# Sample scores of four sequences in one run of four column tiles, and a rearranged start, in a hybrid decoder step

## The chip, the cores and the metric

The kernel runs on one core of a Trainium2 chip, in one launch. The metric is device time in microseconds of one execution; lower is better. The engines are named as in the profile: PE is TensorE (PEld its weight loads), DVE is VectorE, ACT is ScalarE, POOL is GpSimd, SP is SyncE, which only issues DMAs here.

## The reference, cut to what matters

One step of a two-layer decoder for a prompt of 512 tokens and for 8 sample sequences of 4 new tokens each, which have 512 cached positions in pages. D_MODEL is 2048. Layer A runs NSA attention (compressed, selected and window branches) and GLA side by side on one input projection; layer C is HGRN2. Everything is float32.

```python
def layer_a(x, norm_w, w_in, ..., past_kv, win_buf, gla_s0, q_start):
    h = rmsnorm(x, norm_w)
    q, kv, g_br, z_a, q_b, k_b, v_b, lr_b, z_b = split_cols(h @ w_in, A_SIZES)
    ...
    buf = jnp.concatenate([win_buf, new_win], axis=1)
    win_state = buf[:, buf.shape[1] - wb:]
    ...
    o_a = nsa_attend(q, gates, full, win_kv, ...) * jax.nn.silu(z_a)
    log_a = jax.nn.log_sigmoid((lr_b @ gla_w2 + gla_b)) / GLA_GATE_NORM
    ...
    y = x + jnp.concatenate([o_a, o_b], axis=-1) @ w_out
    return y, new_rows, win_state, s_b
```

In `nsa_attend`, for the sample sequences, the selected branch takes all 512 cached positions of the pages (16 blocks of 64) and the window branch the 512 positions of `cache_win`:

```python
        s = jnp.einsum('qgrd,qgnkd->qgrnk', qg, ks)... * scale
        p_s = masked_softmax(s, ...)
        o_s = jnp.einsum('qgrm,qgmd->qgrd', p_s, vs...)
        s = jnp.einsum('qgrd,kgd->qgrk', qg, wk[:, 0]) * scale
        p_w = masked_softmax(s, wmask...)
        o_w = jnp.einsum('qgrk,kgd->qgrd', p_w, wk[:, 1])
```

Besides the two outputs y, the step returns the new cache rows, the window state (for a sample sequence the last 508 rows of `cache_win` and 4 new ones) and the recurrent states.

## The kernel before, in words

**The stream of products.** Prompt and sample tokens stand side by side as 544 columns. `stream` (L296) walks over all weight blocks of the program in one fixed order: the input projection of layer A, its output projection, then the two of layer C. A block has 128 output columns (`gemm_block`, L355) and 16 tiles kt of 128 inputs. Each kt takes six products of 128x272: the weight's high part with the high part of x, with the low part of x, and the weight's low part with the high part of x, each for two halves of the tokens. So a block is 96 products, four pieces of 24. A raw weight tile (`wr`, 512 KB, two pieces) is loaded by a DMA of SP's queue; `split_to` (L314) turns it, some pieces ahead of PE, into `wh` (ACT) and `wl` (DVE). There are NRAW = 3 raw tiles, and a new load is issued as soon as one has been split. Blocks 0 and 1 are interleaved piece by piece; later blocks follow one by one.

**The planner.** All other work is written as Python generators that yield what they wait for. After each kt the stream calls `pump`, and the planner emits what is ready by its own clock. So the order of instructions on each engine is fixed when the program is built; on the chip an engine takes its instructions in that order. Tiles come from a heap of 55 (`self.g`) or from a second pool of 17 that is reopened by stage (`self.r`, `open_r`).

**The start.** `constants` (L409) has POOL build masks. `load_x` (L600) issues five DMAs for a column of 512 of x (four of 128 prompt rows, one of the 32 sample rows); `load0` and `load1` in `layer_a` put the four columns between the first four weight loads, and `small_loads` (L510) puts nine small loads on SP's queue behind the first of them: seven into the tile `cvr` of norm weights and biases, the page table, and `per`. `input_task` (L612) transposes the five tiles of a column on PE in groups (16 kt in all), copies them to `res`, splits them into `xh` and `xl`, and stores `res` to DRAM. The products of piece n of blocks 0 and 1 wait for the flag `xc{n}`, a whole column. `constants2` (L534) transposes `cvr` after the second column.

**Copies of the window cache.** `win_task` (L592) moves 508 rows of `cache_win` to the output for each of 8 sequences: eight DMAs of 1016 KB from DRAM to DRAM, on POOL's queue, the first after the last mask, the others as POOL's order comes to them.

**The first blocks of layer A.** Blocks 0 to 3 are columns of kv; the results of 0 and 1 are copied out and scaled by `rstd` later (`early`), the others wait for `rstd`. Block 4 holds the GLA gate columns; `gl_load` zeroes a raw tile on POOL and fills it with two DMAs of SP's queue, of 1024 runs of 64 and 96 bytes. Meanwhile the compression (`cmp_prep` L1143, `cmp_block` L1184) loads cache pages (`cache_tile` L1125, `pg`), transposes and multiplies them.

**Decode** (L1388) handles the 8 sample sequences in two groups of four, for selected pages (`pg`) and window (`pw`), so four rounds. `fetch` (L1402) keeps up to PAGES = 9 tiles of keys and values on their way. Each round transposes the keys of a sequence and head g to a tile `kct` (128x512) and calls `scores` (L1473): one float32 product with 32 weight columns, `qd`, in the column tile of sequence b % 4:

```python
                self.mm(S[rows, :], self.qd[:, g, b, :], t[:, :TP], start=(g == 0), stop=(g == 1),
                        tile_position=(0, 32 * (b % 4)))
```

PE executes a float32 call as two instructions. A call is emitted one step late (`pend`), between the transposes of the next pair. Softmax, transposes to `ptd` and value products (256 columns, the same four column tiles) follow. After the last round `orow` is transposed into `odec`, and q times z becomes the rows of sample tokens in the inputs of the output projection.

Of the kernel before, what the change touches and what calls it, by code (L numbers as in the profile page):

```python
# [94 lines left out]
class Kern:  # L95
# [200 lines left out]
    def stream(self, blocks, pieces):  # L296

        nc = self.nc
        raws = []
        for b, i, j in pieces:  # L300
            if (b, i) not in raws:
                raws.append((b, i))
        raw_t, hl = {}, {}
        state = {"raw": 0, "free": 0, "split": 0}

        def load():
            while state["raw"] < min(state["free"] + NRAW, len(raws)):
                b, i = raws[state["raw"]]
                t = self.wp.tile([P, 1024], F32, name=self.nm("wr"), tag="wr", bufs=NRAW)
                b.load(i, t)  # L310
                raw_t[(b, i)] = t
                state["raw"] += 1

        def split_to(n):  # L314
            while state["split"] < min(n, len(pieces)):
                b, i, j = pieces[state["split"]]
                w = b.width
                t = raw_t[(b, i)][:, j * w:(j + 1) * w]
                hi = self.wp.tile([P, 512], F32R, name=self.nm("wh"), tag="wh", bufs=4)
                lo = self.wp.tile([P, 512], F32R, name=self.nm("wl"), tag="wl", bufs=4)  # L320
                nc.scalar.copy(hi[:, :w], t)
                self.tt(lo[:, :w], t, hi[:, :w].bitcast(F32), ALU.subtract)
                hl[(b, i, j)] = (hi, lo)
                state["split"] += 1
                if j == 1:
                    del raw_t[(b, i)]
                    state["free"] += 1
                    load()

        load()  # L330
        self.until("xc0")
        late = None
        for n, (b, i, j) in enumerate(pieces):
            split_to(n + 3)
            if i == 0 and j == 0:
                self.until(*(b.needs or ()))
                if b.pre:
                    b.pre()
            if b.ps is None:
                b.ps = self.psum_tile("gm", [P, 2, 512], 2)  # L340
            hi, lo = hl.pop((b, i, j))
            b.products(i * 2 + j, hi, lo, b.ps)
            if late is not None:
                late.evac(late.ps)
                late = None
            if i == b.nraw - 1 and j == 1:
                if b.now:
                    b.evac(b.ps)
                else:
                    late = b  # L350
        if late is not None:
            late.evac(late.ps)
            self.pump()

    def gemm_block(self, w, cols, xhl, evac, order=None, needs=None, ahead=None):  # L355

        nc = self.nc
        order = order or list(range(KT))
        c0, M = cols

        def load(i, t):
            k0 = order[8 * i]
            src = w[k0 * P:(k0 + 8) * P, c0:c0 + M].rearrange("(k p) c -> p k c", p=P)
            nc.sync.dma_start(t[:, :8 * M].rearrange("p (k c) -> p k c", k=8), src)

        def products(n, hi, lo, ps):
            if ahead:
                ahead(n, order)
            for q in range(4):
                kt = order[4 * n + q]  # L370
                xh, xl = xhl(kt)
                wh, wl = hi[:, q * M:(q + 1) * M], lo[:, q * M:(q + 1) * M]
                first, lastk = (n == 0 and q == 0), (n == 3 and q == 3)
                for lw, rx, f, l in ((wh, xh, first, False), (wh, xl, False, False), (wl, xh, False, lastk)):
                    for h in range(2):
                        self.mm(ps[:M, h, :TH], lw, rx[:, h * TH:(h + 1) * TH], start=f, stop=l)
                self.pump()

        return Block(load, 2, 4 * M, products, evac, needs)
# [130 lines left out]
    def small_loads(self):  # L510

        nc, a = self.nc, self.a
        rows = self.g("cvr", [P, P])
        q = nc.sync
        q.dma_start(rows[0:16, :], a["c_norm"].rearrange("o (k p) -> (o k) p", p=P))
        q.dma_start(rows[16:32, :], a["final_norm"].rearrange("(k p) -> k p", p=P))
        q.dma_start(rows[32:64, :], a["c_lb_logits"].rearrange("o (k p) -> (o k) p", p=P))
# [10 lines left out]
    def constants1(self):  # L528

        ps = self.bank()  # L530
        self.tr(ps[:, :16], self.rows0, self.ident[:16, :16])
        self.nc.vector.tensor_copy(self.w_a, ps[:, :16])

    def constants2(self):  # L534

# [55 lines left out]

    def win_task(self):  # L592

        for b in range(NB):
            yield self.later(30000.0)
            self.nc.gpsimd.dma_start(self.o["win_sample"][0, b, 0:508].rearrange("t s h d -> t (s h d)"),
                                     self.a["cache_win"][0, b, 4:512].rearrange("t s h d -> t (s h d)"))


    def load_x(self, c):  # L600

        nc, a = self.nc, self.a
        for i in range(5):
            t = self.g("xt", [P, 512])
            s = slice(c * 512, (c + 1) * 512)
            if i < 4:
                nc.sync.dma_start(t, a["x_prompt"][0, i * P:(i + 1) * P, s])
            else:
                nc.sync.dma_start(t[:TS], a["x_sample"].rearrange("b t d -> (b t) d")[:, s])
            self.xt[(c, i)] = t  # L610

    def input_task(self):  # L612
# [14 lines left out]
        for c in range(4):  # L627
# [5 lines left out]
            for q in range(4):  # L633
# [11 lines left out]
                nc.vector.scalar_tensor_tensor(lo, res, w, hi.bitcast(F32), op0=ALU.mult, op1=ALU.subtract)  # L645
                self.xhl[kt] = (hi, lo)
                self.store(self.xres[kt], res)
            self.flags.add(f"xc{c}")
            yield
            if c:  # L650
# [737 lines left out]
    def decode(self):  # L1388
        nc, ident, a = self.nc, self.ident, self.a
        yield from self.wait("ratt", "gates", "kv10", "kv11", "kvc00", "kvc01", "kvc10", "kvc11")  # L1390
        yield from self.wait(*[f"pu{h}" for h in range(DECODE_AFTER + 1)])
        yield self.at(self.qd)
        self.odec = self.g("odec", [P, 256])
        orow = self.r("orow", [P, 2, P])
# [73 lines left out]
        for gr, kind in items:  # L1468
# [6 lines left out]
                self.mm(S[rows, :], self.qd[:, g, b, :], t[:, :TP], start=(g == 0), stop=(g == 1),  # L1475
                        tile_position=(0, 32 * (b % 4)))

            pend = None
            for b in bs:
                ts = [pages[(kind, 0, b, hf)] for hf in range(2)]  # L1480
                for g in range(2):
                    yield self.at(*ts, banks=1)
                    ps = self.bank()
                    for pg in range(4):
                        self.tr(ps[:, pg * P:(pg + 1) * P], ts[pg // 2][:, pg % 2, g * P:(g + 1) * P], ident)
                    if pend:
                        yield self.at(pend[2], ps)
                    else:
                        yield self.at(ps)
                    t = self.r("kct")  # L1490
                    self.cp(t[:, :TP], ps)
                    if pend:
                        scores(*pend)
                    pend = (b, g, t)
                for hf in range(2):
                    del pages[(kind, 0, b, hf)]
                fetch()
            yield self.at(pend[2])
            scores(*pend)
            pend, t = None, None  # L1500
            yield self.at(S)
            if kind == 1:
                nc.vector.tensor_tensor(S[:, 0:4], S[:, 0:4], self.winneg, op=ALU.add)
# [248 lines left out]
    def layer_a(self):  # L1752
# [10 lines left out]
        blocks = []  # L1763

        def gb(c0, name, done, scale=None, needs=None):
            b = self.gemm_block(w, (c0, P), xhl, self.evac_scaled(name, done, scale), needs=needs)
            blocks.append(b)
            return b

        def gl_load(i, t):  # L1770
            nc.gpsimd.memset(t[:, :512], 0.0)
            v = t[:, :512].rearrange("p (k c) -> p k c", k=8)
            rows = w[i * 1024:(i + 1) * 1024, :]
            nc.sync.dma_start(v[:, :, 0:16], rows[:, OFF_LR:OFF_LR + 16].rearrange("(k p) c -> p k c", p=P))
            nc.sync.dma_start(v[:, :, 32:56], rows[:, OFF_G:OFF_G + 24].rearrange("(k p) c -> p k c", p=P))

        def gl_evac(ps):
            self.gl = self.g("gl")
            nc.vector.tensor_tensor(self.v2(self.gl)[:64], ps[:64, :, :TH], self.v2(self.rstd)[:64], op=ALU.mult)
            self.spawn(self.gates_task())  # L1780
# [97 lines left out]
        heads = [{}, {}, {}, {}]  # L1878
        for n in range(4):
            b = kv_block(n)  # L1880
            if n < 2:
                b.late = (lambda n: lambda t: (self.kT.__setitem__(n, t), self.put("kv", self.kv_out(n, t))))(n)
                early(b)
        gl = self.gemm_block(w, (0, 64), xhl, gl_evac)
# [33 lines left out]
                self.small_loads()  # L1918

        def load1(i, t):  # L1920
            self.load_x(1 if i == 0 else 3)
            x1(i, t)
        blocks[0].load, blocks[1].load = load0, load1
        blocks[0].now = True
        for b in blocks[:2]:
            def products(n, hi, lo, ps, inner=b.products):
                self.until(f"xc{n}")
                inner(n, hi, lo, ps)
            b.products = products
        return blocks  # L1930

    def hgrn_task(self, h, t):
# [83 lines left out]
    def program(self):  # L2016
# [10 lines left out]
        self.spill = spill  # L2027
        nc.real.scalar.preload_act_table_set("natural_log_exp_and_others")
        self.xt, self.xhl = {}, [None] * KT
        self.open_r("rcmp")  # L2030
        self.constants()
        blocks = self.layer_a()

        self.constants1()
        self.put("H", self.input_task(), self.cmp_prep(0, 0, (0, 1)))
        self.spawn(self.constants2())
        self.spawn(self.win_task())
        order_a = list(range(8, 16)) + list(range(8))
# [122 lines left out]
```

## Time and profile before

| | us |
|---|---|
| median of 3 runs | 2357.07 |
| lowest, highest | 2354.96, 2358.32 |
| the profiled execution, its own time | 2358.77 |
| its span, first to last instruction | 2357.1 |
| PE busy | 2312.2 |
| DVE busy | 1397.2 |
| ACT busy | 1008.0 |
| POOL busy | 25.9 |

The mean granted clock of PE over the span is 0.993. The profile moved 270.69 MB, most of it by queue q1 (257.05 MB), which SP feeds; POOL's DMAs are queue q0 (8.32 MB). Times in the trace count from the start of the span. A row of a timeline has its start, its duration, the engine, the line, the operation and the tiles; several instructions of one kind in a row share one row, with their count. The value in brackets is the idle time ahead of the row and what ended it.

### The profile page before, as it was taken

The page shows a single profiled execution, that of the slowest core. Times are in us where ns is not written, and L with a number is a line of the kernel's source. Part 1 is how long each engine was busy: PE and PEld are TensorE (multiplying, and loading weights), DVE is VectorE, ACT ScalarE, POOL GpSimd, SP SyncE. Part 2 cuts the span into 40 slices and gives each one's busy share as a digit, 9 for nine tenths or more (in the row PEclk, how much of TensorE's full clock was granted, in tenths as well). Part 3 has the DMA queues.
Part 4 walks back from the last instruction along what each step waited for, and adds up shares of the span by engine and source line. Part 5 has one row for each costly group of instructions (what it writes and reads, how often), then busy time and mean ns, then how long its engine had stood idle before and what let it go on. Part 6 is the DMA issues. An engine that isn't in the chain of part 4 may idle for free.

```text
span 2357.1 us, 50145 instructions
## 1 busy us (share of the span) xinstructions
PE 2312.2 (98%) x20720; PEld 2234.0 (95%) x20720; DVE 1397.2 (59%) x2999; ACT 1008.0 (43%) x2101; POOL 25.9 (1%) x79
## 2 busy tenths in 40 slices
PE   7799999999999999999999999999999999999997
PEld 7799999999999988879999999999999999999997
DVE  5255567775664653354344777777777777775333
ACT  6244344443442433343333445544444454445333
POOL 3000000000000000000000000000000000000000
PEclk9899999999999999999999999999999999999999
DMA  8755444434213135544443333333333333333333
GB/s 262 232 154 160 126 108 107 115 101 129 55 50 87 46 101 170 153 147 138 137 125 95 99 85 108 105 96 92 99 93 97 97 98 91 93 101 114 105 108 113
DMA packets 433613, 270.69 MB, mean 115 GB/s; under 512 B 16285, under 2 KB 419640, under 8 KB 433256
## 3 DMA queue, kind: packets, MB, share of 16 engines
q1 hardware_dynamic: 432520, 257.05, 37.9%
q0 software_dynamic: 256, 8.32, 1.0%
q8 instruction: 163, 2.67, 0.5%
q10 hardware_dynamic: 608, 2.11, 0.2%
q14 instruction: 66, 0.54, 0.1%
HBM read 234.34 MB, written 41.42 MB: 117 GB/s over the span
## 4 chain that ended last, share of the span: by engine, by line
PE 94%; DVE 1%; DMA 1%; SPq 1%; ACT 1%; issue 0%; DVEq 0%; ACTq 0%
PE gm L211 79%; PE s L211 12%; PE s L215 4%; SPq L84 1%; DVE ol L84 1%; DMA xres<-res 0%; DMA xt<-in_x_prompt_dram 0%; DMA wr<-in_a_w_in_dram 0%; ACT oh L84 0%; DMA pg<-in_cache_kv_dram 0%; ACT e L84 0%; DVE wl L84 0%; DVE e L84 0%; ACT wh L84 0%; DMA out_dram<-snt 0%
## 5 line engine op out<-in xcount | busy, mean ns | idle before, releaser
L211 PE MATMUL gm<-xh,wh 128*128 128x272 f32 x3744 | 803.7, 296 | 1.9 <-ACT wh L84 1.9
L211 PE MATMUL gm<-xl,wh 128*128 128x272 f32 x3744 | 777.4, 289 | 0.1
L211 PE MATMUL gm<-xh,wl 128*128 128x272 f32 x3744 | 775.8, 288 | 1.3 <-DVE wl L84 1.2
L84 DVE TENSOR_TENSOR wl<-wr,wh 128x512 fp32r<-128x512 f32 x660 | 450.4, 686 | 471.2 <-ACT wh L84 470.9
L211 PEld LDWEIGHTS gm<-xh,wh 128*128 128x128 f32 x3744 | 589.3, 189 | 18.1 <-issue 11.8
L84 ACT CAST wh<-wr 128x512 fp32r<-128x512 f32 x660 | 401.9, 616 | 471.7 <-PE gm L211 454.1
L211 PEld LDWEIGHTS gm<-xh,wl 128*128 128x128 f32 x3744 | 588.9, 188 | 2.0 <-DVE wl L84 1.8
L211 PEld LDWEIGHTS gm<-xl,wh 128*128 128x128 f32 x3744 | 589.2, 188 | 0.2
L211 PE MATMUL gm<-oh,wh 128*128 128x272 f32 (+2 forms) x1024 | 218.1, 292 | 2.2 <-ACT oh L84 1.6
L211 PE MATMUL gm<-ol,wh 128*128 128x272 f32 (+2 forms) x1024 | 215.4, 289 | 2.8 <-DVE ol L84 2.7
L211 PE MATMUL gm<-oh,wl 128*128 128x272 f32 (+2 forms) x1024 | 214.3, 288 | 0.0
L211 PEld LDWEIGHTS gm<-ol,wh 128*128 128x128 f32 x1024 | 162.5, 189 | 3.9 <-DVE ol L84 3.9
L211 PEld LDWEIGHTS gm<-oh,wh 128*128 128x128 f32 x1024 | 161.6, 189 | 2.9 <-ACT oh L84 1.9
L211 PEld LDWEIGHTS gm<-oh,wl 128*128 128x128 f32 x1024 | 162.3, 189 | 0.0
L211 PE MATMUL gm<-ch,wh 128*128 128x258 f32 (+1 forms) x256 | 76.9, 300 | 1.3 <-ACT ch L84 1.3
L211 PE MATMUL gm<-cl,wh 128*128 128x258 f32 (+1 forms) x256 | 76.7, 300 | 0.8 <-DVE cl L84 0.8
L211 PE MATMUL gm<-ch,wl 128*128 128x258 f32 (+1 forms) x256 | 76.8, 300 | 0.0
L84 ACT ACTIVATE lv<-lv 128x512 f32<-128x512 f32 (+1 forms) x100 | 61.5, 634 | 29.6 <-DVE lv L84 28.4
L84 ACT COPY o<-s 128x32 f32<-128x32 f32 (+1 forms) x48 | 18.6, 387 | 127.8 <-PE s L211 127.8
L84 ACT ACTIVATE e<-e 128x544 f32<-128x544 f32 x96 | 63.1, 657 | 18.5 <-DVE e L84 16.5
L84 DVE TENSOR_TENSOR lv<-b 128x256 f32<-128x256 f32 (+2 forms) x160 | 68.8, 488 | 0.7
L84 DVE TENSOR_TENSOR rt<-gm,rt 128x544 f32<-128x544 f32 (+2 forms) x33 | 23.3, 707 | 62.0 <-PE gm L211 62.0
(369 smaller groups left out, 2563.2 us busy)
## 6 DMA issues: line engine op xcount, KB each, us to landing
wr<-in_c_w_in_dram SPq DMA_DIRECT2D x128, 512.0 KB
wr<-in_a_w_in_dram SPq DMA_DIRECT2D x104, 512.0 KB
pg<-in_cache_kv_dram SPq DMA_DIRECT2D x128, 128.0 KB
wr<-in_a_cmp_w_dram SPq DMA_DIRECT2D x32, 512.0 KB
wr<-in_a_w_out_dram SPq DMA_DIRECT2D x32, 512.0 KB
wr<-in_c_w_out_dram SPq DMA_DIRECT2D x32, 512.0 KB
out_dram<-s SPq DMA_DIRECT2D x48, 256.0 KB
pw<-in_cache_win_dram SPq DMA_DIRECT2D x32, 256.0 KB
```

The source lines that it names most:

```text
L84: return f(*args, **kw)
L211: return self.nc.tensor.matmul(out, lhsT, rhs, start=start, stop=stop, **kw)
L215: return self.nc.tensor.transpose(out, in_, ident, **kw)
```

## The change

The diff, cut to its core:

```diff
@@ stream @@
-        self.until("xc0")
+        self.until("xk0")
         for n, (b, i, j) in enumerate(pieces):
-            split_to(n + 3)
+            split_to(n + (2 if n < 4 else 3))
@@ gemm_block, products @@
                 kt = order[4 * n + q]
+                if ready:
+                    ready(kt)
@@ small_loads @@
-        q = nc.sync
+        q = nc.gpsimd
@@ constants1 @@
+        ps = self.bank()
+        for k in range(24):
+            self.mm(ps[:, :P], self.onesr, self.onesr)
+        self.nc.vector.tensor_copy(self.sm("warm", [P, 1], bufs=1), ps[:, 0:1])
@@ win_task @@
+        yield from self.wait("rstd2")
         for b in range(NB):
@@ load_x @@
-            t = self.g("xt", [P, 512])
+            t = (self.r if c < 3 else self.g)("xt", [P, 512])
@@ input_task @@
                 self.store(self.xres[kt], res)
+                self.flags.add(f"xk{kt}")
@@ decode @@
-            pend = None
-            for b in bs:
-                ts = [pages[(kind, 0, b, hf)] for hf in range(2)]
-                for g in range(2):
+            for g in range(2):
+                kct = []
+                for b in bs:
+                    ts = [pages[(kind, 0, b, hf)] for hf in range(2)]
...
                     t = self.r("kct")
                     self.cp(t[:, :TP], ps)
-                    if pend:
-                        scores(*pend)
-                    pend = (b, g, t)
-                for hf in range(2):
-                    del pages[(kind, 0, b, hf)]
-                fetch()
+                    kct.append(t)
+                    if g:
...
+                            del pages[(kind, 0, b, hf)]
+                        fetch()
+                yield self.at(*kct)
+                for b, t in zip(bs, kct):
+                    scores(b, g, t)
@@ layer_a @@
+            ready = (lambda kt: self.until(f"xk{kt}")) if len(blocks) < 2 else None
...
-            nc.sync.dma_start(v[:, :, 0:16], rows[:, OFF_LR:OFF_LR + 16].rearrange("(k p) c -> p k c", p=P))
+            nc.gpsimd.dma_start(v[:, :, 0:16], rows[:, OFF_LR:OFF_LR + 16].rearrange("(k p) c -> p k c", p=P))
...
         def gl_evac(ps):
+            self.until("rstd")
...
-            if n < 2:
+            if n < 4:
                 b.late = (lambda n: lambda t: (self.kT.__setitem__(n, t), self.put("kv", self.kv_out(n, t))))(n)
...
         def load1(i, t):
+            x1(i, t)
             self.load_x(1 if i == 0 else 3)
-            x1(i, t)
...
-                self.until(f"xc{n}")
@@ program @@
-        self.open_r("rcmp")
+        self.open_r("rx")
...
-        self.put("H", self.input_task(), self.cmp_prep(0, 0, (0, 1)))
+        self.put("H", self.input_task(), self.call(lambda: self.open_r("rcmp")), self.cmp_prep(0, 0, (0, 1)))
```

In words. The scores of a round are emitted four at a time, for one g, after all four `kct` tiles are there; key tiles are given back while g = 1 is transposed, not after each sequence. The products of blocks 0 and 1 wait for one kt of x, not for a column. The small loads, and the loads of the GLA gate columns, go to POOL's queue; the window copies wait for `rstd2`, which layer C sets. Input tiles of the first three columns come from the second pool. The weight load of block 1 goes ahead of the column of x beside it. 24 products of ones stand ahead of the first transposes. Blocks 2 and 3 are copied out early like 0 and 1, and the GLA block's evacuation waits for `rstd` itself.

What moves, at three places. On PE at the first scores of decode, `s` is a PSUM bank (scores or transposes) and `gm` an input product. Before:

```order
L211 MATMUL s_11617<-kct_11634,qd_10648 32x512
L215 MATMUL s_11692<-ident,pg_11269 128x128 x2
L215 MATMUL s_11692<-ident,pg_11290 128x128 x2
L211 MATMUL gm_11627<-xh_307,wh_11527 128x272 x2
L211 MATMUL gm_11627<-xl_308,wh_11527 128x272 x2
L211 MATMUL gm_11627<-xh_307,wl_11528 128x272 x2
L211 MATMUL s_11617<-kct_11647,qd_10648 32x512
```

After the change, at the same place:

```order
L211 MATMUL gm_11652<-xh_487,wl_11649 128x272 x2
L211 MATMUL s_11642<-kct_11659,qd_10673 32x512
L211 MATMUL s_11642<-kct_11672,qd_10673 32x512
L211 MATMUL s_11642<-kct_11685,qd_10673 32x512
L211 MATMUL s_11642<-kct_11735,qd_10673 32x512
L215 MATMUL s_11753<-ident,pg_11252 128x128 x2
L215 MATMUL s_11753<-ident,pg_11273 128x128 x2
```

One score call between transposes and products has become four in a row, whose outputs lie in four column tiles; the last call of decode stands behind 5850 products of 128x272 instead of 5790, and the output transposes of decode behind 5904 instead of 5856.

On POOL from its last mask on (`esel`). Before:

```order
L84 AFFINE_SELECT esel<-esel 32x128 x2
L84 MEMSET ss_271 128x20
L84 DMA out_dram<-in_cache_win_dram 16x16256
L84 MEMSET wr_857 128x512
L84 DMA out_dram<-in_cache_win_dram 16x16256
L84 MEMSET wr_1028 128x512
L84 DMA out_dram<-in_cache_win_dram 16x16256 x6
L84 MEMSET attT_4177 128x512
```

After the change, the middle and the end of that stretch (seven loads of `cvr` and the page table stand ahead of the first row):

```order
L84 DMA per_272<-in_a_cmp_pe_dram 64x128
L84 MEMSET ss_298 128x20
L84 MEMSET wr_892 128x512
L84 DMA wr_892<-in_a_w_in_dram 128x8x16
L84 DMA wr_892<-in_a_w_in_dram 128x8x24
...
L84 MEMSET attT_16105 128x512
L84 MEMSET attD_16106 128x128
L84 MEMSET ats_16107 32x32
L84 DMA out_dram<-in_cache_win_dram 16x16256 x8
```

The copies of the window cache have moved from between the GLA tiles' memsets to the end of POOL's program, behind the memsets that start layer C; nine small loads and four loads of GLA weights have come in.

On PE at the start, after the change:

```order
L215 MATMUL s_220<-ident,cv_139 128x16
L211 MATMUL s_223<-onesr 128x128 x24
L215 MATMUL s_300<-ident,xt_259 128x32 x4
L215 MATMUL s_305<-ident,xt_251 128x128
...
L215 MATMUL s_305<-ident,xt_257 128x128
L211 MATMUL gm_325<-xh_310,wh_317 128x272 x2
L211 MATMUL gm_325<-xl_311,wh_317 128x272 x2
L211 MATMUL gm_325<-xh_310,wl_318 128x272 x2
L215 MATMUL s_332<-ident,xt_251 128x128
```

Before, the sixteen transposes of the first column stood together ahead of the first product; now the six products of a kt follow the four transposes of that kt. Counted in products of 128x272, the transpose of `cvr` stands at 48 (54 before), the first page transposes at 252 (330 before), and the GLA block's products at 384 to 480 in both.

## Rows read from the trace of the kernel before

**Rows 1.** page of the kernel before: section 1 (busy, share, instructions) and the chain by engine

```profile
PE 2312.2 (98%) x20720; PEld 2234.0 (95%) x20720; DVE 1397.2 (59%) x2999; ACT 1008.0 (43%) x2101; POOL 25.9 (1%) x79
PE 94%; DVE 1%; DMA 1%; SPq 1%; ACT 1%; issue 0%; DVEq 0%; ACTq 0%
```

**Rows 2.** windows: length, then PE, PEld, DVE, ACT, POOL busy, PEclk, DMA, GB/s

```profile
0.00:53.00 53.00, 40.33 (x274) 38.15 (x275) 27.61 (x56) 32.96 (x89) 19.53 (x63) 0.97 0.81 263
20.00:28.00 8.00, 8.00 (x62) 7.60 (x62) 5.04 (x9) 5.19 (x14) 2.86 (x6) 1.00 1.22 411
...
79.70:91.50 11.80, 2.00 (x9) 1.34 (x8) 1.12 (x3) 0.59 (x1) 0.00 (x0) 0.64 0.77 196
91.50:97.00 5.50, 5.50 (x28) 5.49 (x27) 3.61 (x8) 1.29 (x3) 0.00 (x0) 0.54 0.68 207
...
111.00:119.00 8.00, 6.39 (x37) 6.05 (x38) 4.30 (x8) 4.62 (x9) 0.00 (x0) 0.79 0.46 131
```

**Rows 3.** timeline of PE: start, us, engine line, out<-in, count [idle before <-releaser]

```profile
87.57 1.17 PE L215 MATMUL s<-ident,pg 128*128 128x128 f32 x3 [7.83 <-DMA pg<-in_cache_kv_dram]
90.71 1.11 PE L215 MATMUL s<-ident,pg 128*128 128x128 f32 x4 [1.97 <-DVE snt L84]
```

**Rows 4.** timeline of SP's DMA queue, 57 to 90 us

```profile
69.02 15.76 SPq L84 DMA_DIRECT2D wr<-in_a_w_in_dram  x2
```

**Rows 5.** timeline of POOL, 22 to 70 us

```profile
22.18 0.75 POOL L84 DMA_DIRECT2D out_dram<-in_cache_win_dram  x1
...
56.33 0.49 POOL L84 DMA_DIRECT2D out_dram<-in_cache_win_dram  x1
...
64.79 2.88 POOL L84 DMA_DIRECT2D out_dram<-in_cache_win_dram  x6
```

**Rows 6.** DMA queues, 70 to 75 us: packets, MB, share of 16 engines

```profile
q0 software_dynamic: 39, 1.50, 89.1%
q1 hardware_dynamic: 58, 0.05, 4.5%
```

**Rows 7.** DMA queues, 65 to 88 us

```profile
q0 software_dynamic: 192, 6.24, 79.2%
```

**Rows 8.** groups of PE by form: shapes, count | busy, mean ns | idle before

```profile
L211 PE MATMUL s<-kct,qd 128*32 128x512 f32 x64 | 33.1, 604 | 0.0
```

**Rows 9.** timeline of PE in decode, at 877, 918 and 1003 us

```profile
877.59 1.04 PE L211 MATMUL s<-kct,qd 128*32 128x512 f32 x2
...
918.61 1.07 PE L211 MATMUL s<-pg,ptd 128*32 128x256 f32 x16
...
1003.83 1.91 PE L211 MATMUL s<-kct,qd 128*32 128x512 f32 x4
```

**Rows 10.** windows: the end of decode and the start of out_a

```profile
1046.70:1065.00 18.30, 15.78 (x108) 14.90 (x107) 15.24 (x33) 9.93 (x18) 0.00 (x0) 0.91 0.25 78
```

**Rows 11.** timeline of POOL at the start of layer C

```profile
1240.25 0.12 POOL L84 MEMSET ats<- 32x32 f32 x1
```

**Rows 12.** timeline of SP's DMA queue there

```profile
1239.99 6.54 SPq L84 DMA_DIRECT2D wr<-in_c_w_in_dram  x2
```

**Rows 13.** timeline of ACT there

```profile
1251.52 0.62 ACT L84 CAST wh<-wr 128x512 fp32r<-128x512 f32 x1 [0.33 <-PE gm L211]
1254.53 0.62 ACT L84 CAST wh<-wr 128x512 fp32r<-128x512 f32 x1 [2.38 <-PE gm L211]
```

**Rows 14.** timeline of SP's DMA queue, 0 to 24 us

```profile
3.64 0.58 SPq L84 DMA_DIRECT2D cvr<-in_c_norm_dram  x1
...
10.57 2.00 SPq L84 DMA_DIRECT2D xt<-in_x_prompt_dram  x4
```

**Rows 15.** timeline of PE, 8 to 23 us

```profile
8.30 4.24 PE L215 MATMUL s<-ident,xt 32*128 32x32 f32 x20 [4.82 <-DMA xt<-in_x_sample_dram]
```

**Rows 16.** timeline of DVE, 10 to 30 us

```profile
12.11 0.79 DVE L84 TENSOR_SCALAR xh<-res,wa 128x544 fp32r<-128x544 f32 x1
...
25.54 0.49 DVE L84 TENSOR_SCALAR xh<-res,wa 128x544 fp32r<-128x544 f32 x1
```

More of the change, by code (lines that the diff above doesn't have):

```diff
@@ L353, in stream, with gemm_block @@
             self.pump()
-    def gemm_block(self, w, cols, xhl, evac, order=None, needs=None, ahead=None):
+    def gemm_block(self, w, cols, xhl, evac, order=None, needs=None, ahead=None, ready=None):
         nc = self.nc
@@ L1391, in decode @@
         yield from self.wait(*[f"pu{h}" for h in range(DECODE_AFTER + 1)])
+        self.khl = None
         yield self.at(self.qd)
@@ L1485, in decode @@
                         self.tr(ps[:, pg * P:(pg + 1) * P], ts[pg // 2][:, pg % 2, g * P:(g + 1) * P], ident)
-                    if pend:
-                        yield self.at(pend[2], ps)
-                    else:
-                        yield self.at(ps)
+                    yield self.at(ps)
                     t = self.r("kct")
                     self.cp(t[:, :TP], ps)
-                    if pend:
-                        scores(*pend)
-                    pend = (b, g, t)
-                for hf in range(2):
-                    del pages[(kind, 0, b, hf)]
-                fetch()
-            yield self.at(pend[2])
-            scores(*pend)
-            pend, t = None, None
+                    kct.append(t)
+                    if g:
+                        del ts
+                        for hf in range(2):
+                            del pages[(kind, 0, b, hf)]
[3 more added lines that the diff above has]
+                    scores(b, g, t)
+                t, kct, ts = None, None, None
             yield self.at(S)
@@ L1765, in gb @@
         def gb(c0, name, done, scale=None, needs=None):
-            b = self.gemm_block(w, (c0, P), xhl, self.evac_scaled(name, done, scale), needs=needs)
+            ready = (lambda kt: self.until(f"xk{kt}")) if len(blocks) < 2 else None
+            b = self.gemm_block(w, (c0, P), xhl, self.evac_scaled(name, done, scale), needs=needs, ready=ready)
             blocks.append(b)
@@ L1773, in gl_load @@
             rows = w[i * 1024:(i + 1) * 1024, :]
-            nc.sync.dma_start(v[:, :, 0:16], rows[:, OFF_LR:OFF_LR + 16].rearrange("(k p) c -> p k c", p=P))
-            nc.sync.dma_start(v[:, :, 32:56], rows[:, OFF_G:OFF_G + 24].rearrange("(k p) c -> p k c", p=P))
+            nc.gpsimd.dma_start(v[:, :, 0:16], rows[:, OFF_LR:OFF_LR + 16].rearrange("(k p) c -> p k c", p=P))
+            nc.gpsimd.dma_start(v[:, :, 32:56], rows[:, OFF_G:OFF_G + 24].rearrange("(k p) c -> p k c", p=P))
         def gl_evac(ps):
+            self.until("rstd")
             self.gl = self.g("gl")
@@ L1920, in load1 @@
         def load1(i, t):
+            x1(i, t)
             self.load_x(1 if i == 0 else 3)
-            x1(i, t)
         blocks[0].load, blocks[1].load = load0, load1
         blocks[0].now = True
-        for b in blocks[:2]:
-            def products(n, hi, lo, ps, inner=b.products):
-                self.until(f"xc{n}")
-                inner(n, hi, lo, ps)
-            b.products = products
         return blocks
```

## The prediction, made before the changed kernel ran

> **What bounds the kernel now.** I read the page first: TensorE is busy for 2312.2 of 2357.1 us, and the chain that ended last is PE for 94% [rows 1]. So a change pays in two ways only: fewer PE microseconds, or fewer of the 45 us in which PE stands idle and of those in which its clock is low. Next I read the windows by stage, to find where PE stands. Between 79.7 and 91.5 us PE is busy for 2.00 of 11.80 us; 91.5 to 97 is full, but at a granted clock of 0.54; 111 to 119 lacks 1.61 us and has 0.79 [rows 2]. Against the upper level, 2.4 GHz, that is 9.8 + 0.7, 2.5 and 1.6 + 1.3 us: some 15.9 us lost in one stretch. The waits say for what: transposes of cache pages stand 7.83 us for a page and then 1.97 us for VectorE [rows 3].
>
> Why the page is late is told by the queues. SP issues two loads over 15.76 us from 69.02 on, so it is stuck [rows 4]. GpSimd has just issued six cache_win copies in a row, at 64.79 [rows 5]. In 70 to 75 us the copies' queue q0 has the DMA engines for 89.1% of the time and everything else, q1, for 4.5%; the counts are 39 and 58 packets [rows 6]. A weight load is cut into 1024 runs of 512 bytes, so at one or two packets of q1 for one of q0 hardly anything of q1 passes while copies run. The six copies' 192 packets take 79.2% of 23 us: 18.2 us, or 3.04 us a copy [rows 7].
>
> **The change, part by part** (against the profiled span of 2357.1 us; that execution took 2358.77, 1.7 above the median of 2357.07, so the span stands for the median and I add nothing).
>
> 1. Scores in four column tiles. The 32 calls are 64 instructions of 33.1 us [rows 8]. A lone call takes 1.04 us, and a pair in one run 1.91 [rows 9]: one column tile after another, a further call costs 0.87. What several tiles cost together is in the value products: sixteen instructions with half the columns (256), in four tiles, take 1.07 us in all [rows 9], no more than one tile's share of them alone. Four calls of 512 columns in four tiles should then take the time of one, 1.04. Eight such runs: 8.3 us, **−24.8**. The other end is four calls that still go one by one, 1.04 + 3 x 0.87 = 3.65 a run, 29.2 in all, so −3.9. I take the first: the value products have the same tiles and the same type. The kct tiles wait for copies and pages, but PE has input products between them.
>
> 2. What is late next. Scores in runs end later among the products, so the last group's output transposes move 48 products, 6.0 us, to just ahead of the output products that need them. Before, that end lost 2.5 us of idle time and 9% of clock over 18.3 us [rows 10], 4.2 us together. Now the transposes, odec, the split and q run with nothing beside them; by the same instructions some 2.9 us. **0**, from −1 to +3.
>
> 3. cache_win copies off the first 100 us. They now wait for rstd2, which is layer C's start. The stretch of 15.9 us loses its cause. But page transposes stand 78 products earlier in PE's order, so pages are needed some 10 us sooner, which may keep half of the wait. Ends −15.9 and −8; **−15**, since SP is free at once without the copies.
>
> 4. The same eight copies at layer C. They follow GpSimd's last memset, at 1240.25 [rows 11], and have no other wait, so all eight go at once: 8 x 3.04 = 24.3 us, until about 1265. A weight load that SP issues at 1239.99 [rows 12] then lands when they end, plus 2.7 us (512 KB at the 196 GB/s of 79.7 to 91.5, [rows 2]), at about 1267.4. ScalarE's casts come every 3.01 us, a piece of 24 products [rows 13]; with three raw tiles a load is issued eight pieces ahead of PE, less 1.4 us for its split, so that PE runs out at 1262.7. It stands 4.7 us and then loses some 2.4 by a low clock, as after the stall of rows 3. **+7**; 0 if this load passes ahead of the copies and the later ones catch up, +12 if two loads are caught.
>
> 5. The start. Nine small loads leave SP's queue, where they stand from 3.64 us on and the second column of x only at 10.57 [rows 14]; x comes up to 7 us sooner. Input tiles from the other pool need not wait for stores of xres. But of PE's 12.7 idle us ahead of 53 [rows 2] only 4.4 lie behind the first transposes, which wait for x until 8.30 anyway [rows 15]. Against it, the tile of constants is now loaded by GpSimd, whose first free moment is 22.18 [rows 5]: seven issues of 0.48 (2.88 / 6, [rows 5]) make 25.5, and, landing some 2 us later, they come just where PE's order wants them. **−3**, between −7 (all x early) and +4 (a late tile). The 24 warm-up products lie ahead of 8.30, where PE only waits: 0.
>
> 6. The two GLA weight tiles. Four loads of 1024 short runs each go to GpSimd, which no row shows. The first can be issued at about 53.3 us (56.33 [rows 5], less the 3 us of part 5), and PE reaches product 384, which needs the second tile, at about 86 us (before, it stands from 79.7 on [rows 2] with 330 products done; 54 more at 0.125). If an issue costs what a copy's costs (0.48), both tiles are some 25 us early: 0. If GpSimd pays by the run, a copy's 32 runs in 0.48 make p = 15.4 us for a load, and with 3 us of landing PE stands 53.3 + 4p + 3 − 86 = 4p − 29.7 = 32 us. I take **0**, the issue rows being the nearest of that engine.
>
> Two more blocks evacuated early and the second wait for rstd move work of VectorE and ScalarE, 59% and 43% busy [rows 1]: 0.
>
> The sum: −24.8 + 0 − 15 + 7 − 3 + 0 = −35.8, so **2321 us**.
>
> **A rule against part 5.** While GpSimd works, VectorE's xh takes 0.79 us, and 0.49 once it has stopped at 22 us [rows 16]: one slows the other. VectorE is busy for 5.04 of 8 us in 20 to 28 us [rows 2], so an issue could take 0.48 / (1 − 0.63) = 1.3 us; the constants would land at 33.3 us rather than 27.5, and PE, which keeps its order, would stand 6 us: 2327. The Trainium skill (SBUF — State Buffer, "SBUF: two separate sides") states a harder rule: a DMA issued from GpSimd waits for a lock while VectorE copies, and 620 ns become 3100. An estimate by that page's figure is seven issues until 44 us, a stand of 18 us and about 2339. The trace does not bear it out so far: the copy issued at 22.18, amid VectorE's work, took 0.75 us [rows 5].
>
> **The rivals.**
> (a) The copies at layer C harm nothing, since weights already loaded suffice, and the start gains its full 7 us: 2357.1 − 24.8 − 15.9 + 0 − 7 = 2309. For it: loads run eight pieces ahead. Against it: rows 6 show q1 all but stopped, for the whole of a burst.
> (b) GpSimd starved by VectorE, as just worked out: 2327. Rows 5 speak against more.
> (c) Column tiles don't overlap at 512 columns: −3.9 for −24.8, 2342. The value products speak against it.
> (d) The other side: GpSimd pays by the run for the GLA loads, and product 384 waits for the fourth. With p = 15.4 the kernel takes 2353; it is slower than now from p = 16.4 us. Slowed by VectorE as well (0.79 / 0.49, a factor of 1.6) p is 24.6, the stand 69 us and the time 2390. For it: these loads have 32 times the runs of a copy. Against it: no row shows that an issue's time grows with its runs.
> (e) As (d) with p from 9.5 to 12.5: 8 to 20 us late, 2329 to 2341.
>
> **How the numbers follow.** The forecast has 0.62, (a) 0.15, (b) 0.09, (c) 0.04, (d) 0.06, (e) 0.04. The bounds of the parts added up give −24.8 − 1 − 15.9 + 0 − 7, 2308, at one end and −24.8 + 3 − 8 + 12 + 4, 2343, at the other; not all come together. The range **2308 to 2342** takes in (a), (b), (c) and (e) and leaves out (d) and some of the sums of bad ends, 0.12 in all. A measurement of this kernel tells 0.2%, 4.7 us, from no change. All cases but (d) are faster by more: 0.94. Of (d) 0.02 lies within it, 0.04 beyond.
>
> **What would show it.** In the changed profile: 64 score instructions in runs of eight of about 1.05 us; no PE wait of over 2 us for a page before 100 us; eight copies in a row from about 1205 us on (1240 less what is gained before), q0 at some 90% there, and one PE wait of 4 to 5 us for a weight within 25 us; the seven constant loads issued by 26 us; GLA loads of half a microsecond each. The prediction is wrong if the runs of eight last over 3 us, if PE waits for GLA weights or constants, or if a wait like the 7.83 us stays with no copy beside it.

## The result and the profile after

The changed kernel takes 2324.82 us (median of 4 runs, 2322.59 to 2326.81); the kernel before, run beside it, 2356.02. The ratio is 0.9866, 95% interval [0.9849, 0.9883]. The medians differ by 31.2 us. The profiled span is 2322.4 us, 34.7 less than the 2357.1 of before: the profiled execution of before (2358.77) lay 2.75 us above this median, that of the change (2324.13) 0.7 below. 2321 had been forecast.

GpSimd's memsets mark the same places of the program in both kernels, so the span can be cut into four stages:

| stage, ended by | before, us | after, us | difference |
|---|---|---|---|
| start and compression, first memset of attT | 307.41 | 293.67 | −13.7 |
| GLA and prompt attention, memset of qd | 499.38 | 499.46 | +0.1 |
| decode and out_a, second memset of attT | 432.85 | 405.76 | −27.1 |
| layer C, end of the span | 1117.46 | 1123.51 | +6.0 |

Each column is one execution. In e1_decode_only, which runs the code of before in the first stage and in layer C, these took 303.36 and 1120.7 us, 4.05 less and 3.2 more than here. So a difference of 3 or 4 us in one stage, read from two profiles, can be chance.

The page of the changed kernel, busy time, and the group of PE by form that answers to [rows 8]:

```profile
PE 2288.0 (99%) x20744; PEld 2231.0 (96%) x20744; DVE 1394.5 (60%) x2998; ACT 1012.1 (44%) x2105; POOL 33.5 (1%) x92
```
```profile
L211 PE MATMUL s<-kct,qd 128*32 128x512 f32 x64 | 8.5, 605 | 0.0
```

The same 64 instructions sum to 8.5 us, not 33.1. In PE's timeline a run of eight lasts 1.07 us. The instruction behind a group of four transposes starts 0.41 us after the group where that group follows a run of scores, and 0.35 us after it where it follows products:

```profile
870.08 1.07 PE L211 MATMUL s<-kct,qd 128*32 128x512 f32 x8
871.08 0.66 PE L215 MATMUL s<-ident,pg 128*128 128x128 f32 x4
871.49 0.50 PE L211 MATMUL gm<-xh,wh 128*128 128x272 f32 x2
...
872.33 0.60 PE L215 MATMUL s<-ident,pg 128*128 128x128 f32 x4
872.68 0.50 PE L211 MATMUL gm<-xh,wh 128*128 128x272 f32 x2
```

The windows of the first stage (columns as in [rows 2]): the hole of 9.8 us is gone, and small waits come later.

```profile
0.00:53.00 53.00, 45.24 (x309) 42.00 (x310) 26.38 (x57) 35.33 (x89) 23.03 (x71) 1.00 0.78 239
53.00:80.00 27.00, 26.80 (x218) 26.35 (x217) 13.29 (x32) 10.34 (x24) 4.63 (x6) 1.00 0.67 174
80.00:100.00 20.00, 20.00 (x165) 19.97 (x164) 6.75 (x12) 6.74 (x13) 0.00 (x0) 1.00 0.55 157
100.00:130.00 30.00, 29.33 (x242) 28.73 (x241) 18.05 (x39) 14.10 (x27) 0.00 (x0) 1.00 0.61 174
130.00:294.00 164.00, 159.66 (x1199) 157.21 (x1198) 80.84 (x142) 64.26 (x114) 0.33 (x1) 1.00 0.47 140
```

The waits of PE in 100 to 300 us (total, times, longest), after:

```profile
PE s L215 <- DMA pg<-in_cache_kv_dram: 4.8, 6, 1.5
```

Before, waits for pages cost 2.0 us there, two in number. GpSimd's timeline, the lines that answer to [rows 5, 11]:

```profile
21.42 0.74 POOL L84 DMA_DIRECT2D cvr<-in_c_norm_dram  x1
...
24.77 0.51 POOL L84 DMA_DIRECT2D cvr<-in_a_cmp_b_dram  x1
...
57.17 1.82 POOL L84 DMA_DIRECT2D wr<-in_a_w_in_dram  x2 [0.29 <-POOL wr L84]
...
1199.51 0.12 POOL L84 MEMSET ats<- 32x32 f32 x1
1199.57 3.94 POOL L84 DMA_DIRECT2D out_dram<-in_cache_win_dram  x8
```

Behind the eight copies DMA looks in 1200 to 1226 us like [rows 6]. A weight load that SP issues at 1205.43 lands 26.32 us later (chain that ended last); PE stands for its split and then runs at a low clock (timeline of PE, windows):

```profile
q0 software_dynamic: 238, 8.19, 88.9%
q1 hardware_dynamic: 1206, 0.61, 9.4%
```
```profile
1205.43 26.32 DMA wr<-in_c_w_in_dram
```
```profile
1232.51 0.82 PE L211 MATMUL gm<-xh,wh 128*128 128x272 f32 x2 [3.46 <-ACT wh L84]
```
```profile
1232.60:1239.00 6.40, 6.40 (x29) 6.40 (x30) 3.56 (x6) 2.14 (x4) 0.00 (x0) 0.52 0.53 154
```

3.46 us of idle time and 6.40 at a granted clock of 0.52, so 3.1 more, are 6.5, about the 6.0 that the fourth stage lost.

### The profile page after: what moved, and what is told of

Same layout as the page of the kernel before. It is cut to its first block, busy times and chain, and to the rows that moved or that the text cites. A ratio compares the mean times of both kernels' runs of the same rounds, so it can differ in the third digit from the quotient of the medians.

```text
span 2322.4 us, 50208 instructions
## 1 busy us (share of the span) xinstructions
PE 2288.0 (99%) x20744; PEld 2231.0 (96%) x20744; DVE 1394.5 (60%) x2998; ACT 1012.1 (44%) x2105; POOL 33.5 (1%) x92
## 4 chain that ended last, share of the span: by engine, by line
PE 93%; DMA 2%; ACT 1%; POOL 1%; DVE 1%; issue 1%; SPq 1%; DVEq 0%; POOLq 0%; ACTq 0%
PE gm L211 79%; PE s L211 11%; PE s L215 4%; DMA wr<-in_c_w_in_dram 1%; DMA pg<-in_cache_kv_dram 1%; SPq L84 1%; ACT junk L84 0%; DVE ol L84 0%; POOL mkt L84 0%; ACT wh L84 0%; POOL cvr L84 0%; ACT oh L84 0%; ACT e L84 0%; ACT res L84 0%; POOL lmb L84 0%
## 5 line engine op out<-in xcount | busy, mean ns | idle before, releaser
L84 DVE TENSOR_TENSOR lv<-b 128x256 f32<-128x256 f32 (+2 forms) x160 | 68.9, 488 | 0.7
```

What stands on the lines that cost most here:

```text
L84: return f(*args, **kw)
```

## The experiments

The theory is the sum of the prediction; each run tests one of its terms. A ratio is to the kernel before, run beside it, with its 95% interval. The mark for the start is dg, PE's product of the tile dg with ones, which ends the norm of x. Before and after the change (timeline of PE):

```profile
59.71 1.39 PE L211 MATMUL s<-dg,ones 128*128 128x128 f32 x10
```
```profile
56.85 1.39 PE L211 MATMUL s<-dg,ones 128*128 128x128 f32 x10
```

The first stands behind 240 input products, the second behind 228; at 0.1254 us a product (3.01 for 24, [rows 13]) the first is 58.20 at 228. Two runs that share the start of the change, e3_copies_spread and e4_two_tiles, have dg at 57.29 and 56.44, so a few tenths of a microsecond mean nothing.

**Decode alone** (e1_decode_only), in the kernel before:

```diff
 (decode of the change, all else as before)
```

> The kernel before with the new decode alone: scores of four sequences in a run, everything else as before. My theory (four column tiles work at once): score rows of 8.5 us in all instead of 33.1, and the stretch from the memset of qd to the start of layer C, 432.8 us before and 405.8 in the change, falls to about 406; total about 27 us less, near 2330. Rival (the calls still go one by one, and the time went elsewhere): score rows of about 29 us and a total within 5 us of before.

2331.45 us, ratio 0.9893 [0.9878, 0.9908]. The score rows sum to 8.5 us and the third stage is 404.8 (432.85 before), so decode gives its 27 to 28 us there by itself; the total falls by 25.3. The early stall stays (waits of 4.97, 2.65 and 1.93 us at 83 to 89 us).

**Two tiles instead of four** (e4_two_tiles), in the changed kernel:

```diff
-            for g in range(2):
-                kct = []
-                for b in bs:
+            for two in (bs[:2], bs[2:]):
+                for g in range(2):
+                    kct = []
+                    for b in two:
```

> The changed kernel with scores in runs of two sequences, so two column tiles in a run instead of four, sixteen runs. If the tiles of a run work at once, a run takes as long as one call, about 1.05 us, and the score rows sum to 16.9 us, twice the 8.5 of the change; total near 2333. If a run had a fixed cost and the calls in it were nearly free for another reason (fewer switches between transposes and scores), the sum would lie near 8.5 + 8 x 0.1 = 9.3 us and the total within 2 us of the change.

2332.26, ratio 0.9896 [0.9879, 0.9912]. The group by form, and a run:

```profile
L211 PE MATMUL s<-kct,qd 128*32 128x512 f32 x64 | 16.8, 605 | 0.0
```
```profile
863.61 1.05 PE L211 MATMUL s<-kct,qd 128*32 128x512 f32 x4
```

33.1, 16.8 and 8.5 us with one, two and four tiles in a run: a run costs 1.04 to 1.07 us whatever its tiles. Two calls in one tile took 1.91 in the kernel before: the pair of [rows 9] is the last two of a round, g = 0 and g = 1 of one sequence. So the time went by tiles working at once, not by fewer switches. The Trainium skill (TensorEngine Tiling (Array Packing), "Theoretical Speedup") gives up to 4x where the small dimension is 32 or less; the trace has 3.9 (33.1 to 8.5).

**The copies alone moved** (e2_copies_late), in the kernel before:

```diff
     def win_task(self):
+        yield from self.wait("rstd2")
```

> The kernel before with one line more: the window copies wait for rstd2. My theory (the copies alone starve pages and weights): the wait of 7.83 us for a page and the low clock after it vanish, 10 to 16 us gained before 300 us; and 5 to 7 us lost within 41 us after the start of layer C, by one PE wait for a weight and a stretch at a low clock; together 5 to 10 us faster, near 2348. Rival (the early page wait comes from the order of loads on SP, the small loads and GLA loads in it): the wait for a page stays at 5 us or more, and the total is not faster.

2350.32, ratio 0.9971 [0.9960, 0.9981]. The first stage takes 295.46, 11.95 less than before (7.9 less than in e1_decode_only), with no page wait over 1.2 us; layer C takes 1122.7, 5.2 more, with one PE wait of 2.59 us for a weight. Both halves are as expected, but a wait of 2.56 us for a compression weight at 110 us is new.

**The copies spread over layer C** (e3_copies_spread), in the changed kernel (a small GpSimd copy of a head's tile stands ahead of each, at heads 1, 3 to 15):

```diff
+        g = self.sm("wg", [P, 1], bufs=1)
+        self.nc.gpsimd.tensor_copy(g, x[:, 0:1])
         self.nc.gpsimd.dma_start(self.o["win_sample"][0, b, 0:508]...
```

> The changed kernel, with each of the eight copies behind a small GpSimd copy of a tile that a later head of layer C gives (heads 1, 3 and so on to 15), so one copy in about 100 us instead of eight at once. My theory (the burst costs 6 us at the start of layer C): the PE wait of 3.46 us for wh and the half clock after it vanish, and the total falls by about 6 us, to near 2319. Rival (the wait comes from layer C's own loads beside x1res, or each single copy costs as much as an eighth of the burst): the wait stays, or comes back as eight small ones, and the total stays within 2 us of the changed kernel.

2320.39, ratio 0.9843 [0.9829, 0.9857], an interval that overlaps that of the change; layer C takes 1119.0 us, 4.5 less than in the change, without a wait for a weight. One copy at a time costs PE nothing that its waits show.

**The copies early again** (e5_copies_early), in the changed kernel:

```diff
     def win_task(self):
-        yield from self.wait("rstd2")
```

> The changed kernel without its wait for rstd2, so the eight window copies go out early again, two behind the small loads at about 27 us and six behind the loads of the GLA weights. My theory (the copies starve pages and weights in the first 130 us): waits of PE of 8 us or more in all for pages or GLA weights come back between 60 and 130 us, layer C starts without its 3.46 us wait, and the total is 4 to 10 us over the change, near 2332. Rival (the other edits of the start removed the stall): waits for pages before 130 us stay under 2 us, and the total is 6 us under the change, near 2319.

2324.01, ratio 0.9863 [0.9847, 0.9880]: neither. Layer C is back at 1117.7, but the first stage takes only 297.49, 3.8 more than in the change. The two copies at 26 us delay dg to 62.45 us with 246 products done, 60.19 at 228 (56.85 in the change): 3.3 of the 3.8. The six at 69 us cost hardly more. They stop SP's queue as before: of the four loads in the second row of SP's timeline one alone takes 12.80 us to issue.

```profile
56.74 8.75 SPq L84 DMA_DIRECT2D pg<-in_cache_kv_dram  x8
...
73.58 18.78 SPq L84 DMA_DIRECT2D pg<-in_cache_kv_dram  x4
```

But the pages of the first transposes go out by 65.5, ahead of the burst at 69.03, and the first that PE waits for behind it, 0.73 us, is at 96.02 (timeline of PE):

```profile
96.02 1.11 PE L215 MATMUL s<-ident,pg 128*128 128x128 f32 x6 [0.73 <-DMA pg<-in_cache_kv_dram]
```

So a burst alone does not make the stall. The times fit a second condition, a page asked for inside the burst: before, SP's eight page loads stood at 58.95 to 68.9, the burst at 64.79. No run moved the pages alone, so this condition is read from the times and not tested. The copies' move alone takes 11.95 us from the first stage, the other edits alone 9.9, both 13.7; against the 303.36 of e1_decode_only these are 7.9, 5.9 and 9.7.

**No warm-up products** (e6_no_warm), in the changed kernel:

```diff
-        for k in range(24):
-            self.mm(ps[:, :P], self.onesr, self.onesr)
```

> The changed kernel without the 24 products of ones ahead of the first transposes; the rest of PE's order is the same. As I predicted it (they lie where PE only waits): the product of dg with ones starts within 0.7 us of its 56.4 to 57.3 in the runs with them. Rival (they bring the clock up sooner): input products at half rate last beyond 16.4 us, and dg starts 1.5 to 3 us later.

2325.29, ratio 0.9868 [0.9851, 0.9884]. dg stands at 57.25. The first transposes start at 7.98 instead of 8.68, since the warm-up lasts past the arrival of x; the clock comes up about a microsecond later, at 17.6. The two about cancel.

**Columns instead of tiles** (e9_by_column), in the changed kernel:

```diff
-            ready = (lambda kt: self.until(f"xk{kt}")) if len(blocks) < 2 else None
+            ready = (lambda kt: self.until(f"xc{kt // 4}")) if len(blocks) < 2 else None
```

> The changed kernel, with blocks 0 and 1 waiting for a whole column of x again (four kt) instead of for one. If products tile by tile save time, the product of dg with ones starts 1 to 3 us later than the 56.4 to 57.3 us of the change. If the start is set by the arrival of x and weights (my theory after the first four runs, in which the old start without a copy at 22 us stood no later than the new one), it starts within 1 us.

2321.9, ratio 0.9852 [0.9835, 0.9868]; dg at 56.75. Products tile by tile gain nothing that shows.

**Small loads back on SP** (e7_small_on_sp), in the changed kernel:

```diff
-        q = nc.gpsimd
+        q = nc.sync
```

> The changed kernel with the nine small loads on SP's queue again, behind the first column of x. If they hold x back there, as I predicted (7 us on the queue), dg starts 1 us or more later than the 56.4 to 57.3 us of the change. If the start does not hang on the second column (rival), dg starts within 1 us, and the total stays within 2 us of the change.

2322.88, ratio 0.9854 [0.9839, 0.9869]; dg at 57.16. The rival holds.

**GLA loads back on SP** (e8_gla_on_sp), in the changed kernel:

```diff
-            nc.gpsimd.dma_start(v[:, :, 0:16], ...
+            nc.sync.dma_start(v[:, :, 0:16], ...
```

> The changed kernel with the four loads of the GLA gate columns on SP's queue again. If they cost PE nothing on either queue, as I predicted, the memset of attT that ends this part starts within 1.5 us of the 292.6 to 294.0 of the kernels with them on GpSimd's queue. Rival (4096 short runs on SP's queue hold pages back): waits for pages grow by 3 us or more, and that memset starts 3 us or more later.

2327.17, ratio 0.9877 [0.9862, 0.9892]; the memset at 294.14, page waits of 5.7 us in all (5.0 in the change). No difference that the first stage shows.

**The old start** (e10_old_start) with decode and spread copies, so the new start by itself:

```diff
 (decode of the change and win_copy of e3_copies_spread, all else as before)
```

> The kernel before with two parts alone: decode in runs of four, and the copies spread over layer C as in e3_copies_spread. The start, the small loads, the GLA loads and the early blocks are as before. If the new start is worth nothing by itself (dg stood at 57.16 us with 240 products done in e2_copies_late, which is 55.65 at 228, against 56.4 to 57.3 in the kernels with the new start), the total is within 2 us of e3_copies_spread, 2318 to 2321. If the new start saves the 3 us that I predicted, the total is 2322 or more.

2321.44, ratio 0.9849 [0.9833, 0.9866], 1 us from e3_copies_spread. dg stands at 56.62 with 240 products done, 55.11 at the 228 of the change. The new start is worth nothing in the total; by this mark it is 1.7 us late (2.2 in e3_copies_spread). The first stages still end alike, 294.39 here and 294.04 in e3_copies_spread, for the old order loses lead again later, in part by a wait for a compression weight (2.56 us in e2_copies_late), whose load SP issues at 102.43, behind eight page loads:

```profile
108.88 0.39 PE L211 MATMUL gm<-ch,wh 128*128 128x258 f32 x1 [2.05 <-ACT wh L84]
```

The kernels with the new start have no such wait there.

**Where the new start is held.** SP's timeline of the change has the last column of x behind stores of xres and a weight load:

```profile
10.33 2.68 SPq L84 DMA_DIRECT2D xt<-in_x_prompt_dram  x4
13.46 0.33 SPq L84 DMA_DIRECT2D xt<-in_x_sample_dram  x1
14.16 0.38 SPq L84 DMA_DIRECT2D wr<-in_a_w_in_dram  x1
15.01 5.98 SPq L84 DMA_DIRECT2D xres<-res  x5
28.45 0.38 SPq L84 DMA_DIRECT2D wr<-in_a_w_in_dram  x1
28.89 2.00 SPq L84 DMA_DIRECT2D xt<-in_x_prompt_dram  x4
```

In e12_x_first it goes right behind the third (copies spread, too):

```diff
             self.load_x(0 if i == 0 else 2)
+            if i:
+                self.load_x(3)
             x0(i, t)
```

> The changed kernel with the copies spread as in e3_copies_spread, and the last column of x issued right behind the third, ahead of the weight loads and of the stores of xres that stand before it on SP's queue in the change (there it goes out at 28.89 us, with DMA idle from about 23 to 29 us). My theory (the new start loses what it gains because this column is late): no PE wait for xt or for ACT behind it at 36 us, dg starts at 56.5 us or sooner with 246 products done (18 more than in the change, 2.3 us of work, so 54.3 or sooner against 56.4 to 57.3), and the total is 1 to 3 us under e3_copies_spread, 2317 to 2320. Rival (splits and weights hold the start): dg, corrected for the 18 products, stays within 0.7 us of the change, and the total at 2320 or above.

2318.93, ratio 0.9840 [0.9826, 0.9853]. The wait for x is gone, but dg, corrected, is at 57.45: PE now waits 1.25 us for the constants, then 0.91 for a weight, and the products behind run at half rate (0.45 us from a pair to the next at 29.83, 0.25 elsewhere):

```profile
28.04 0.26 PE L215 MATMUL s<-ident,cvr 75*128 75x75 f32 x1 [1.25 <-DMA cvr<-in_a_cmp_b_dram]
29.21 0.82 PE L211 MATMUL gm<-xh,wh 128*128 128x272 f32 x2 [0.91 <-ACT wh L84]
```

The theory fails for dg; a new wait has taken the place of the old. The last run (e13_x_first_sp) takes that away:

```diff
-        q = nc.gpsimd
+        q = nc.sync
...
             x0(i, t)
-            if i == 0:
+            if i:
                 self.small_loads()
```

> e12_x_first with the nine small loads on SP's queue, behind the fourth column of x and the third weight load, so that PE transposes the constants 42 products later and does not wait for GpSimd (1.25 us, and a low clock behind it, in e12_x_first). If that wait is what holds the start now, dg (at 204 products here, 24 fewer than in the change, 3.0 us of work) starts at 52.5 us or sooner, and the total is 1 to 2 us under e12_x_first, 2316.5 to 2318. Rival (splits of x and weights on ScalarE and VectorE hold the start, whatever the order of loads): dg, corrected for the products, stays at 56.2 to 57.5, and the total within 1 us of e12_x_first.

2317.35, ratio 0.9828 [0.9815, 0.9842], the lowest; its interval lies below that of the changed kernel and overlaps those of e3_copies_spread and e12_x_first. dg starts at 51.55, so 54.56 at 228 products:

```profile
34.84 0.23 PE L215 MATMUL s<-ident,cvr 75*128 75x75 f32 x1
```
```profile
51.55 1.39 PE L211 MATMUL s<-dg,ones 128*128 128x128 f32 x10
```

But the first stage ends at 293.67, as in the change (293.06 in e12_x_first): what the start gains is spent later in the stage, and the 1.6 us between the totals of the last two runs do not come from it. That the total fell as expected is luck. Where the gain goes (waits for pages of 4.1 us stay) is open.

## Why the prediction was right

The sum, −35.8, was near the −34.7 of the spans; the medians gave −31.2. The mechanisms of its three large terms were right in the main: scores in column tiles, the early stall, the burst at layer C. Two terms were credited to the wrong edits. That the sum is so near is in part luck: the first stage gave 13.7 of the 18 forecast (15 and 3), decode with out_a 27.1 of 24.8, layer C took 6.0 of 7, and these misses nearly cancel.

- **Scores, −24.8.** Measured −24.6 (33.1 to 8.5), by tiles at once, as the value products of [rows 9] had said. The pair of 1.91 that priced rival (c) has one tile and says nothing of several. The stage gave 27.1. Of the other 2.5 some 1.0 us fits transposes that now stand behind products (0.35 us to the next instruction, not 0.41, for 17 of the 32 groups); that share was not tested by itself, and the rest is open.
- **The end of decode, 0.** Right: in 20 us around it PE stands 2.18 us, 2.52 before, at a clock of 0.91 both times. The longest wait there is 1.94 us for a split (1.88 before).
- **The early stall, −15.** The stall went, and small waits for pages kept a part: 4.8 us for 2.0 after 100 us. The term was too large: the first stage's 13.7 less the 1.35 of the start is 12.4, and against e1_decode_only the whole stage gave 9.7. And "copies off the first 100 us" was not the only key: e5_copies_early shows that the other edits also remove the stall. I had the burst as cause, and overlooked that the new order sends the pages before it.
- **The copies at layer C, +7.** Measured +6.0: q0 at 88.9%, 3.46 us of idle time and 3.1 by the clock, against 4.7 and 2.4. PE ran out some 7 us later than I had worked out (1229.05, which is 1269.8 on the clock of before, not 1262.7), so the wait came 29.5 us behind the first copy and not within 25. The load issued at 1199.24, 0.3 us ahead of the copies, was not the one that PE stood for; the next, issued at 1205.43, was, and landed only at 1231.74.
- **The start, −3.** A mis-sized term, and its cause was wrong. (The idle time behind the first transposes was 1.89 + 1.20 + 1.54 = 4.6 us, not 4.4.) dg came 1.35 us sooner at equal products (58.20 to 56.85). But the old start gives 56.79 in e1_decode_only, with the copy at 22 us as before, and without that copy 55.65 (e2_copies_late) and 55.11 (e10_old_start): the copy cost some 1 to 3 us, and the new order gives some 1 to 2 back (56.44 to 57.29 in the runs with it), part of it by the last column of x and the constants. Small loads, tiles and warm-up each move dg by 0.4 us or less, no more than unchanged starts differ.
- **GLA loads, 0.** A load of 1024 runs issues in 0.91 us (1.82 for two), near twice the half microsecond expected, but not in the 15.4 of a price by the run: rivals (d) and (e) fall, and PE has no wait for these weights.
- **The rule against part 5.** The seven loads took 0.50 to 0.74 us each while VectorE was busy for 3.88 of 4.90 us (21.4 to 26.3). So rival (b), 1.3 us a load, falls. Its premise is not borne out here either: VectorE's xh took 0.50 us at 15.82, beside GpSimd's masks, and 0.50 at 22.16 and 24.09, beside the issues. The Trainium skill (SBUF — State Buffer, "A bandwidth-pool intuition that's wrong (but worth ruling out)") gives its 3100 ns for a load beside a VectorE `tensor_copy`; in 21.4 to 26.3 us VectorE ran no copy, so no run here shows that case. But GpSimd's order had no slack: 1.25 us in e12_x_first.

## What to carry to other kernels

Products with few output rows in different column tiles should be issued back to back: here a run of one, two or four took the same time, and a profile shows in its own rows of that shape whether they overlap. Long DRAM-to-DRAM copies did least harm here one by one beside steady work, not in a burst; where a burst must be, ask which load is issued behind it and how soon it is needed. A stall removed by two edits at once belongs to neither: undo each alone before crediting it, and take more than one profile of the kernel before, since one execution's first stage differed from another's by 4 us.

## What the runs showed of the hardware

Eight copies of 1016 KB on one queue took 88.9% of the DMA engines' time in 1200 to 1226 us and left 9.4% to SP's queue. A weight load issued at 1205.43 took 26.32 us to land, and the issue of a later one lasted 12.05 us, where one ahead of the copies (1199.24) took 0.37:

```profile
1218.39 12.05 SPq L84 DMA_DIRECT2D wr<-in_c_w_in_dram  x1
```

Float32 score calls of 32 rows and 512 columns took 1.91 us for two calls in one column tile (before), 1.05 for two in two tiles (e4_two_tiles) and 1.07 for four in four (the change).

The issue time of a DMA on GpSimd grew from 0.49 us at 32 packets (a copy, [rows 7]) to 0.91 at 1024 runs, far less than their number.
